# First norm by a root per quarter, delta-rule features by halves, differential attention's projections ahead of the grouped ones

## Chip, core and metric

The kernel runs on one core of a Trainium2 chip. The metric is the device time of one execution in microseconds; of three executions the median counts. TensorE is called PE here, VectorE DVE, ScalarE ACT, GpSimd POOL, and SP is the engine that issues all DMAs.

## What is computed

Two layers of a diffusion block with four mixers side by side, on 512 latent and 256 context tokens (768 in all) of width 1024, batch 1, in float32. The reference, cut to one layer:

```
mod_l = split(silu(c) @ mod_w + mod_b, 6);  mod_c likewise from c_ctx
h = rms_norm(x, g) * (1 + scale) + shift            # latent and context
pa, pb, pc, pd = split(h @ w_in)                    # 1152, 768, 800, 512 columns
oa = rwkv7_mixer(pa)     # delta rule, 4 heads of 64, both directions, context first
ob = diff_attention(pb)  # softmax(q1 k1) - lam * softmax(q2 k2), 4 heads, rope, norms
oc = gla_mixer(pc)       # gated linear attention in chunks of 64, both directions
od = gqa_mixer(pd)       # 4 query heads on 2 key heads
x = x + gate * (concat(oa, ob, oc, od) @ w_out)
x = x + gate2 * conv_ffn(modulate(x))               # 2816 wide, 3-tap convolution
```

The second layer gives no context output.

## The kernel before

Tokens lie along the free axis and features on the 128 partitions: x is eight blocks [128, 768]. Large products run as three products of rounded halves (high x high, high x low, low x high); `weights` (line 366) loads pieces of 512 KB into a ring of three stages, ACT rounds them (line 378) and POOL subtracts for the low half (line 379). All scratch in SBUF comes from 30 slabs of 1536 columns that `Arena` hands out while the program is being written: a [768] tile is half a slab. PSUM has eight banks, handed out in the same way.

The program of a layer is written by generators that `weave` (line 300) runs in turns: each yields an amount of time, scaled by PACE, and the one with the least goes next. For the mixers these are `rwkv` (delta rule), `gla`, `attentions`, `projections`, and in layer 0 `mod_mix`, the later modulation vectors. A generator may also wait for a flag (`wait`) or for whole free slabs (`room`). A scheduler then orders the instructions of each engine, so code order is not queue order; each engine takes its queue in order.

- **Start** (`start`, line 1840): x is loaded block by block, squared on ACT, and summed over the width by 48 products with the square as the weights and one column of ones (line 1849). The modulation vectors of shift and scale come in eight pairs; pair m is what block m of the norm needs (`mod_first`, `mod_pair`: line 466 the products on four column groups, line 470 the turn). `norm` calls pair m right before block m, then computes block m: DVE line 619, ACT line 621, and for the low half DVE line 623, or, for blocks 1, 4 and 7, ACT line 626 and POOL line 628. The first feature projections (line 388) follow block by block.
- **Projections** (line 756): gated linear attention's, the delta rule's, then the grouped keys and values, grouped queries, and differential keys, values and queries (line 748, per token tile 24 products). Raw keys, queries and values are spilled to DRAM (line 810). At the end h is freed and the flag "h free" is set.
- **Attentions**: `begin` (line 1041) waits for the kind's flag and for "h free", makes rope tables, loads six key tiles (line 936), turns them (POOL lines 884, 886, 890, DVE 887, 891), splits them (ACT 903, DVE 904) and transposes them on PE (line 428). Then scores (line 979, grouped 982), maximum (DVE 985), exponential (ACT 987), transposes and values (line 1015), unit by unit: differential pair 0, pair 1, grouped.
- **Delta rule**: `front(d)` waits for four whole slabs, then computes for each half p (two heads) the features (`features`: products with the small matrices at line 1390, DVE 1393 to 1416), into one slab KB with keys and b side by side and one slab RA. When both halves are there, `blocks` makes the 64x64 blocks per chunk pair (line 1434, ACT 1440, scratch writes 1443), and KB and RA are dumped (lines 1505, 1507). `inverses` (DVE 1463, 1465) works on the scratch; `direction` loads the dumps (1474, 1476) and runs `rw_prep` (line 1590) and `rw_chain` (1708, 1713) over six chunk pairs, whose POOL step is line 1622.

## Time and profile before

| what | value |
|---|---|
| median of three runs | 2402.65 us (2399.67 to 2406.67) |
| the profiled execution | 2396.04 us |
| its span, first to last instruction | 2394.1 us |
| PE busy | 2219.6 us (93%) |
| DVE, POOL, ACT busy | 1320.7, 994.7, 937.3 us |
| mean granted PE clock | 0.951 |
| PE line 388 (three-product projections, feed-forward) | 1235.9 us |
| PE line 748 (token projections) | 250.6 us |

The places of the two layers in the span: start to 82 us; projections of layer 0 to 382.7 us; its mixers to 755 us; output projection, feed-forward and the next norm to 1407 us; projections of layer 1 to 1701 us; mixers to 1973 us; the rest to the end.

A busy PE is one whose queue has a product under way; how fast it goes depends on the granted clock, which is given as a share of full speed. A wait is shown in brackets behind an instruction, with the engine and line that ended it. In the timeline the x counts are records: a product of float32 operands in one pass pair leaves two.

### The profile page before, as it was taken

To read this page: it belongs to the slowest core of one execution; us is meant where nothing else is said; L and a number is where in the kernel's file an instruction comes from. 1 tells how busy PE (TensorE), PEld (TensorE's weight loads), DVE (VectorE), ACT (ScalarE), POOL (GpSimd) and SP (SyncE) were. 2 spreads that over 40 slices of the span, in tenths; PEclk is the share of its full clock that TensorE was granted. 3 is DMA by queue.
4 is the path that set the end of the run, shared out by engine and by line. 5 is a ranking of instruction groups with operands and counts; after the bars stand their busy time and mean duration, and the time that the engine had idled before them with its cause. 6 is when DMAs were issued, how large, how long until landed. Compare 5 with 4: busy or idle time off the path is not lost. (4 is left out here: it accounts for less than half of the span.)

```text
span 2394.1 us, 40730 instructions
## 1 busy us (share of the span) xinstructions
PE 2219.6 (93%) x15684; PEld 1876.6 (78%) x15684; DVE 1320.7 (55%) x2902; ACT 937.3 (39%) x1762; POOL 994.7 (42%) x994
## 2 busy tenths in 40 slices
PE   7989995888989999999999989997899889999999
PEld 6778794767767788888888878777778668888888
DVE  2133567686784498555544662368767875332323
ACT  3333232545566342323223344322266474433333
POOL 1343445222431253434344545345442414655556
PEclk8999997789999999999999999998899899999999
DMA  6522254332324244333423432135533232333334
GB/s 217 202 80 85 80 178 119 94 76 63 84 88 146 86 133 130 112 107 115 141 93 102 150 103 65 56 96 143 124 92 80 60 124 80 97 97 97 97 97 133
DMA packets 228978, 258.52 MB, mean 108 GB/s; under 512 B 90608, under 2 KB 173872, under 8 KB 228784
## 3 DMA queue, kind: packets, MB, share of 16 engines
q1 hardware_dynamic: 228784, 255.92, 35.5%
q8 instruction: 123, 2.02, 0.3%
q14 instruction: 71, 0.58, 0.1%
HBM read 209.69 MB, written 37.77 MB: 103 GB/s over the span
## 5 line engine op out<-in xcount | busy, mean ns | idle before, releaser
L388 PE MATMUL pst<-slab,slab 128*128 128x512 f32 (+1 forms) x6552 | 1235.9, 350 | 13.1 <-POOL slab L628 5.4
L388 PEld LDWEIGHTS pst<-slab,slab 128*128 128x128 f32 x6552 | 1047.1, 190 | 196.0 <-POOL slab L628 10.0
L379 POOL TENSOR_TENSOR slab<-slab,slab 128x512 fp32r<-128x512 f32 (+1 forms) x428 | 566.6, 1333 | 718.4 <-ACT slab L378 686.7
L378 ACT CAST slab<-slab 128x512 fp32r<-128x512 f32 (+1 forms) x428 | 258.6, 612 | 570.7 <-PE pst L388 414.3
L748 PE MATMUL pst<-slab,slab 128*128 128x256 f32 (+1 forms) x1872 | 250.6, 293 | 4.2 <-POOL slab L379 4.0
L748 PEld LDWEIGHTS pst<-slab,slab 128*128 128x128 f32 x1872 | 239.6, 197 | 13.4 <-POOL slab L379 5.4
L428 PE MATMUL pst<-cst,slab 128*128 128x128 f32 (+1 forms) x968 | 170.1, 309 | 70.7 <-POOL slab L1622 23.9
L661 DVE SCALAR_TENSOR_TENSOR slab<-pst,pp,slab 128x511 f32<-128x511 f32 x66 | 41.6, 657 | 299.7 <-ACT slab L658 299.7
L428 PEld LDWEIGHTS pst<-cst,slab 128*128 128x128 f32 (+1 forms) x968 | 122.6, 155 | 100.7 <-POOL slab L1622 25.6
L1590 PE MATMUL pst<-slab,slab 128*128 128x128 f32 (+4 forms) x1328 | 162.8, 284 | 10.7 <-DMA slab<-kb 2.6
L1590 PEld LDWEIGHTS pst<-slab,slab 128*128 128x128 f32 (+3 forms) x1328 | 135.0, 180 | 33.0 <-issue 9.7
L692 DVE SCALAR_TENSOR_TENSOR slab<-pst,fgate,slab 128x512 f32<-128x512 f32 (+1 forms) x144 | 88.2, 628 | 108.0 <-PE pst L388 107.9
L985 DVE TENSOR_REDUCE mx<-pst 128x1 f32<-128x768 f32 (+1 forms) x120 | 100.1, 845 | 41.6 <-PE pst L979 27.2
L987 ACT ACTIVATE slab<-pst,mx 128x768 f32<-128x768 f32 (+1 forms) x120 | 97.8, 816 | 38.9 <-DVE mx L985 37.2
L532 DVE SCALAR_TENSOR_TENSOR slab<-slab,slab 128x512 bf16<-128x512 f32 x128 | 110.2, 861 | 4.7 <-DMA slab<-in_modw_dram 3.0
L673 POOL TENSOR_TENSOR slab<-slab,slab 128x768 fp32r<-128x768 f32 (+1 forms) x44 | 74.1, 1685 | 65.4 <-ACT slab L672 65.4
L1015 PE MATMUL pst<-slab,slab 128*64 128x128 f32 x832 | 67.7, 294 | 9.0 <-DVE slab L425 5.1
L998 ACT ACTIVATE slab<-slab,r 128x768 f32<-128x768 f32 (+1 forms) x80 | 67.1, 851 | 11.8 <-DVE r L997 11.6
L1015 PEld LDWEIGHTS pst<-slab,slab 128*64 128x64 f32 x832 | 48.0, 143 | 23.5 <-DVE slab L425 7.5
L672 ACT CAST slab<-slab 128x768 fp32r<-128x768 f32 (+1 forms) x44 | 32.1, 729 | 82.5 <-DVE slab L669 82.4
L667 ACT ACTIVATE slab<-slab 128x768 f32<-128x768 f32 (+1 forms) x44 | 32.5, 738 | 80.0 <-DVE slab L663 79.9
L1622 POOL TENSOR_TENSOR slab<-slab,pc 128x256 f32<-128x256 f32 x48 | 32.2, 686 | 67.8 <-PE pst L1708 14.6
(312 smaller groups left out, 2657.8 us busy)
## 6 DMA issues: line engine op xcount, KB each, us to landing
slab<-in_wup_dram SPq DMA_DIRECT2D x88, 512.0 KB, 3.7
slab<-in_modw_dram SPq DMA_DIRECT2D x112, 256.0 KB, 3.0
slab<-in_wdn_dram SPq DMA_DIRECT2D x48, 512.0 KB, 3.5
slab<-in_win_dram SPq DMA_DIRECT2D x46, 512.0 KB, 3.6
slab<-in_modp_dram SPq DMA_DIRECT2D x40, 512.0 KB, 5.1
slab<-in_wout_dram SPq DMA_DIRECT2D x16, 512.0 KB, 3.6
slab<-in_xT_dram SPq DMA_DIRECT2D x16, 384.0 KB, 5.0
kb<-slab SPq DMA_DIRECT2D x8, 768.0 KB, 4.0
```

What stands on the lines that cost most here:

```text
L378: nc.scalar.copy(out=w[0], in_=st[:, k:k + q])
L379: nc.gpsimd.tensor_tensor(out=w[1], in0=st[:, k:k + q], in1=w[0].bitcast(F32), op=ALU.subtract)
L388: self.nc.tensor.matmul(ps[:, a:b], w[i][k][:, cols], x[j][k][:, a:b], start=(k == 0 and q == 0), stop=(k == nk - 1 and q == 2))
L428: self.nc.tensor.transpose(out, a.bitcast(F32) if a.dtype != F32 else a, self.c["ident"])
L532: self.tc.keep_in_program_order(nc.vector.scalar_tensor_tensor(out=junk, in0=w, scalar=1.0, in1=self.sc[s][e], op0=ALU.mult, op1=ALU.mult, ...
L673: nc.gpsimd.tensor_tensor(out=HL[:, 1, :n], in0=th[:, :n], in1=HL[:, 0, :n].bitcast(F32), op=ALU.subtract)
L692: nc.vector.scalar_tensor_tensor(out=x[m][:, a:b], in0=ps[:, a:b], scalar=gate[:, m, s:s + 1], in1=x[m][:, a:b], op0=ALU.mult, op1=ALU.add)
L748: self.nc.tensor.matmul(ps[:, :n], h[i][k][:, t * P:(t + 1) * P], w[j][k], start=(k == 0 and q == 0), stop=(k == KD - 1 and q == 2))
L985: nc.vector.tensor_reduce(out=mx, in_=sv, axis=AX.XY, op=ALU.max, negate=True)
L987: nc.scalar.activation(out=p[m][:, a:].rearrange("p (e c) -> p e c", e=2 - a // hb), in_=sv, func=AF.Exp, bias=mx, accum_out=lsum[:, m:m + 1])
L1015: nc.tensor.matmul(acc[64 * e:64 * e + 64, :P], vs[e][:, i + j], aT[:, 256 * j + P * e:256 * j + P * e + P], start=(first and j == 0), sto ...
L1590: mm = lambda o, a, b, pos: nc.tensor.matmul(o, a, b, start=True, stop=True, tile_position=pos)
```

## The change

Four parts.

1. `start` sums the squares with 32 columns of ones as weights and the square moving, one product per quarter of the tokens, each on its own column group. `mod_first` runs all eight modulation pairs before the norm, with four pairs of buffers instead of three, and the first two projection weights are asked for before them. `root_first` computes the root on [128, 192] and spreads it with four products. For the other norms the same code as before moved into `root`.
2. `front` waits for nine free half slabs of which two are whole (`halves`), and does one half p after the other: features into four separate [768] tiles, blocks of this half, dumps of this half, and frees them.
3. `projections` does differential keys, values and queries first and the grouped ones last.
4. `begin` no longer waits for "h free"; the first one waits for five whole slabs.

```diff
-    ROOM = ((4, 7, 4, 2), (4, 7, 4, 2))
+    ROOM = (((9, 2), 7, 4, 2), ((9, 2), 7, 4, 2))
...
     def mod_first(self):
-        ws = [[self.new([4, 256]) for _ in range(2)] for _ in range(3)]
+        n = 4
+        ws = [[self.new([4, 256]) for _ in range(2)] for _ in range(n)]
...
+        self.early.update({q: self.win(0, q, 0, KD) for q in EARLY})
+        for m in range(KD):
+            ps = yield from self.bank(1, 2, 4)
+            self.mod_pair(m, [ws[m % n][k // 4][:, k % 4] for k in range(KD)], ps)
+            self.free(ps)
+            if m + n < KD:
+                load(m + n)
+        self.free(*sum(ws, []))
+
+    def root_first(self, ps):
+        n = T // 4
...
+        ms, r, t1, t2 = (self.new([n]) for _ in range(4))
+        nc.vector.tensor_scalar(out=ms, in0=ps[:, :n], scalar1=1.0 / D, scalar2=EPS, op0=ALU.mult, op1=ALU.add)
+        self.rsqrt(r, ms, t1, t2)
+        rb = yield from self.bank(4, 4, 8)
+        for g in range(4):
+            nc.tensor.matmul(rb[:, 512 * g:512 * g + n], first[32 * g:32 * g + 32], r[32 * g:32 * g + 32], start=True, stop=True,
+                             tile_position=(32 * g, 0))
+        rs = self.new([T])
+        nc.scalar.copy(out=rs.rearrange("p (g c) -> p g c", g=4), in_=rb.rearrange("p (g c) -> p g c", g=4)[:, :, :n])
...
-        for kind, hd, nh, nk, blocks in (("gq", 64, 4, 2, ("gqkv", "gqq")), ("da", 32, 8, 8, ("dak", "dav", "daq"))):
+        for kind, hd, nh, nk, blocks in (("da", 32, 8, 8, ("dak", "dav", "daq")), ("gq", 64, 4, 2, ("gqkv", "gqq"))):
...
+    def halves(self, n, slabs):
+        for _ in range(100000):
+            last, m = self.arena.last, Arena.SLAB // 2
+            free = [np.isfinite(last[:, q:q + m]).all(axis=1) for q in (0, m)]
+            whole = free[0] & free[1]
+            part = np.array([k == F32 for k in self.arena.kind])
+            if (whole * 2).sum() + ((free[0] ^ free[1]) & part).sum() >= n and whole.sum() >= slabs:
+                break
+            yield 100
...
-            yield from self.wait(S, kind + " ready", "h free")
+            yield from self.wait(S, kind + " ready")
+            if before is None:
+                yield from self.room(5)
...
-            nc.vector.tensor_tensor(out=KBp[:, :, 0:4:3], in0=ch2(tb), in1=ch2(ip), op=ALU.mult)
+            nc.vector.tensor_tensor(out=bx, in0=tb, in1=ip, op=ALU.mult)
...
-            nc.vector.tensor_tensor(out=KBp[:, :, 1:3], in0=ch2(th), in1=ch2(ip), op=ALU.mult)
+            nc.vector.tensor_tensor(out=kx, in0=th, in1=ip, op=ALU.mult)
...
+        def blocks(d, p, bx, rx):
+            ps = yield from self.bank(2, *self.RB[d])
+            for j in range(NT):
                 for hl in range(2):
+                    for u in range(2):
+                        nc.tensor.matmul(ps[U(u), 512 * hl + 64 * j:512 * hl + 64 * j + 64], rx[U(hl), j * P + 64 * u:j * P + 64 * u + 64],
+                                         bx[U(hl), j * P + 64 * u:j * P + 64 * u + 64], start=True, stop=True, tile_position=(64 * hl, 64 * u))
+            for hl in range(2):
+                ab = self.new([NT, 64])
+                nc.scalar.copy(out=ab.rearrange("p j t -> p (j t)"), in_=ps[:, 512 * hl:512 * hl + 64 * NT])
...
         def front(d):
-            KB[d], RA[d] = [], []
-            yield from self.room(self.ROOM[li][0])
             for p in range(2):
-                KB[d].append(self.new([NT, 4, 64]))
-                RA[d].append(self.new([2, T]))
-                yield from features(d, p)
+                yield from self.halves(*self.ROOM[li][0])
+                kx, bx, rr, rx = (self.new([T]) for _ in range(4))
+                yield from features(d, p, kx, bx, rr, rx)
+                yield from blocks(d, p, bx, rx)
...
+                nc.sync.dma_start(out=self.kb[d][:, :, p, 64:192], in_=kx.rearrange("p (j c) -> p j c", j=NT))
+                for u in range(2):
+                    nc.sync.dma_start(out=kbd[:, :, 3 * u], in_=c2(bx)[:, :, u])
+                for e, (a, m) in enumerate(((rr, nt), (rx, NT))):
+                    nc.sync.dma_start(out=self.ra[d][:, :m, p, e], in_=a[:, :m * P].rearrange("p (j t) -> p j t", j=m))
+                self.free(kx, bx, rr, rx)
...
-            ps = yield from self.bank(1, 4, 5)
+            ps = yield from self.bank(1, 0, 1)
...
-                for t in range(NT):
-                    nc.tensor.matmul(ps[:, t:t + 1], v[:, t * P:(t + 1) * P], self.c["ones"][:, 0:1],
-                                     start=(k == t == 0), stop=(k == KD - 1 and t == NT - 1))
+                for g in range(4):
+                    nc.tensor.matmul(ps[32 * g:32 * g + 32, 0:T // 4], self.c["ones"][:, 0:32], v[:, T // 4 * g:T // 4 * (g + 1)],
+                                     start=(k == 0), stop=(k == KD - 1), tile_position=(0, 32 * g))
...
-            yield from self.norm(0, "nmg", x, [st], h, [self.spans(True)], first)
+            yield from self.mod_first()
+            yield from self.norm(0, "nmg", x, [{}], h, [self.spans(True)], ps)
```

How the queues are ordered. PE at the start, before: line 1849 are the sums, 466 and 470 the modulation pairs, 604 the spread of the root, 388 the projections.

```order
L466 MATMUL pst<-slab_16_180,slab_5_100 32x256 x4
L466 MATMUL pst<-slab_17_181,slab_5_100 32x256 x4
L604 MATMUL pst<-slab_13_108,cst 128x512
L604 MATMUL pst<-slab_13_108,cst 128x256
L470 MATMUL pst<-cst,slab_5_100 128x2 x2
L466 MATMUL pst<-slab_18_182,slab_5_100 32x256 x4
L466 MATMUL pst<-slab_19_183,slab_5_100 32x256 x4
L466 MATMUL pst<-slab_20_184,slab_5_100 32x256
L470 MATMUL pst<-cst,slab_6_101 128x2 x2
L466 MATMUL pst<-slab_20_184,slab_5_100 32x256 x3
L466 MATMUL pst<-slab_21_185,slab_5_100 32x256 x4
L388 MATMUL pst<-slab_27_240,slab_1_96 128x512
```

PE at the same place, after (lines 1879, 470, 474, 514 and 392 are the same steps):

```order
L474 MATMUL pst<-cst,slab_7_102 128x2 x2
L470 MATMUL pst<-slab_18_166,slab_5_100 32x256 x4
L470 MATMUL pst<-slab_19_167,slab_5_100 32x256 x4
L474 MATMUL pst<-cst,slab_16_164 128x2 x2
L470 MATMUL pst<-slab_20_168,slab_5_100 32x256 x4
L514 MATMUL pst<-slab_6_101,slab_5_100 128x192 x4
L470 MATMUL pst<-slab_21_169,slab_5_100 32x256 x4
L474 MATMUL pst<-cst,slab_16_164 128x2 x2
L470 MATMUL pst<-slab_22_170,slab_5_100 32x256 x4
L392 MATMUL pst<-slab_25_319,slab_1_96 128x512
L392 MATMUL pst<-slab_25_319,slab_2_97 128x512
L392 MATMUL pst<-slab_25_319,slab_1_96 128x256
```

The spread of the root moved from behind the second pair to the middle of the seventh, and no projection stands before it.

SP in layer 0, before, from the spill of the last projected block: rawdaq is the spill of differential queries (line 810), slab<-rawdak a load of a key tile (line 936), scrin, kb and ra the delta rule's scratch and dumps.

```order
L810 DMA rawdaq<-slab_8_103 128x1536
L1480 DMA slab_6_101<-scrin_400 64x4x64 x2
L936 DMA slab_20_184<-rawdak 128x128 x2
L1505 DMA kb_89<-slab_17_181 768x1x256
L1507 DMA ra_91<-slab_16_180 768x1x128
L936 DMA slab_39_463<-rawdak 128x128
L1507 DMA ra_91<-slab_16_180 768x1x128
L936 DMA slab_98_3681<-rawdaq 128x128
L1676 DMA slab_108_3823<-slab_6_101 64x64 x4
L936 DMA slab_39_463<-rawdak 128x128
L1676 DMA slab_108_3823<-slab_6_101 64x64 x3
L936 DMA slab_98_3681<-rawdaq 128x128
```

SP in layer 0, after; rawgqq is the spill of the grouped queries (line 832), now the last block:

```order
L969 DMA slab_5_100<-rawdak 128x128
L1471 DMA scrin_388<-slab_6_101 64x6x64 x2
L1471 DMA scrin_388<-slab_33_385 64x6x64 x2
L969 DMA slab_7_102<-rawdak 128x128
L969 DMA slab_18_166<-rawdak 128x128
L1509 DMA slab_18_166<-scrin_387 64x4x64
L969 DMA slab_10_105<-rawdak 128x128
L969 DMA slab_90_3485<-rawdaq 128x128
L969 DMA slab_33_385<-rawdak 128x128
L969 DMA slab_115_3904<-rawdaq 128x128
L1509 DMA slab_21_169<-scrin_387 64x4x64
L832 DMA rawgqq<-slab_13_108 128x1536
```

The loads of the second to sixth key tile stand before that spill, behind the scratch writes of the second direction's first half.

PE in layer 1, before, around the last projection product (line 748); 1590, 1708 and 1713 are the delta rule's, 428 transposes of keys, 979 scores.

```order
L1590 MATMUL pst<-slab_16_180,slab_6_101 64x64 x7
L748 MATMUL pst<-slab_331_7199,slab_316_6633 128x256
L1708 MATMUL pst<-slab_385_12345 64x64 x4
L1590 MATMUL pst<-slab_356_10595,slab_35_398 64x128 x4
L1708 MATMUL pst<-slab_385_12345 64x64 x4
L1713 MATMUL pst<-slab_6_101,slab_373_11747 64x64 x4
L1590 MATMUL pst<-slab_18_182,slab_356_10595 128x128 x4
L1590 MATMUL pst<-slab_380_12310,slab_20_184 128x128 x4
L1590 MATMUL pst<-slab_356_10595,slab_18_182 128x64 x8
L428 MATMUL pst<-cst,slab_380_12310 128x2x64 x4
L428 MATMUL pst<-cst,slab_356_10595 128x128 x2
L1590 MATMUL pst<-slab_20_184,slab_376_12099 64x64 x8
```

PE in layer 1, after, where the first scores stand (line 1012); 770 are projections, 1620 the delta rule's.

```order
L770 MATMUL pst<-slab_330_7175,slab_314_6604 128x256
L432 MATMUL pst<-cst,slab_390_13745 128x128 x4
L1012 MATMUL pst<-slab_388_13736,slab_390_13745 128x384
L1012 MATMUL pst<-slab_389_13737,slab_390_13745 128x384
L1012 MATMUL pst<-slab_388_13736,slab_390_13745 128x384
L1012 MATMUL pst<-slab_389_13737,slab_390_13745 128x384 x2
L1012 MATMUL pst<-slab_388_13736,slab_390_13745 128x384
L1620 MATMUL pst<-slab_322_6989 128x64 x4
L1012 MATMUL pst<-slab_388_13736,slab_390_13745 128x384
L1012 MATMUL pst<-slab_389_13737,slab_390_13745 128x384
L770 MATMUL pst<-slab_212_5540,slab_315_6605 128x256
L770 MATMUL pst<-slab_329_7170,slab_315_6605 128x256
```

The last key transposes and the first scores stand in front of projection products, of which 168 more follow.

## Rows read from the trace of the kernel before

**Rows 1.** windows of the span; "x" are records, then clock, DMA share, GB/s:

```profile
core 0: us, PE busy (x) PEld busy (x) DVE busy (x) ACT busy (x) POOL busy (x), PEclk, DMA share, GB/s
10.00:15.00 5.00, 5.00 (x26) 5.00 (x25) 0.00 (x0) 1.68 (x2) 0.00 (x0) 1.00 1.03 413
28.50:82.00 53.50, 45.59 (x281) 28.47 (x281) 21.33 (x61) 20.51 (x43) 10.86 (x8) 0.84 0.59 202
382.70:433.00 50.30, 19.49 (x137) 14.56 (x138) 30.83 (x67) 10.52 (x25) 27.85 (x47) 0.56 0.38 110
433.00:755.00 322.00, 279.60 (x2616) 228.11 (x2617) 236.30 (x627) 183.48 (x402) 88.68 (x145) 0.92 0.34 92
755.00:1407.00 652.00, 640.57 (x3604) 553.91 (x3603) 390.04 (x734) 198.82 (x311) 275.24 (x189) 0.98 0.38 119
1595.50:1660.00 64.50, 47.79 (x433) 42.66 (x432) 46.90 (x93) 21.55 (x52) 43.06 (x45) 0.88 0.52 149
1701.00:1759.00 58.00, 46.27 (x306) 37.16 (x301) 37.88 (x105) 23.21 (x51) 21.78 (x43) 0.74 0.40 100
1759.00:1973.00 214.00, 196.87 (x1929) 161.29 (x1924) 160.95 (x393) 134.76 (x270) 67.09 (x114) 0.94 0.32 88
```

**Rows 2.** timeline of PE at the start (start us, us, instruction, wait):

```profile
7.92 20.64 PE L1849 MATMUL pst<-cst,slab 128*128 128x1 f32 x96 [7.92 <-ACT slab L1847]
...
76.98 1.82 PE L388 MATMUL pst<-slab,slab 128*128 128x512 f32 x8 [2.32 <-POOL slab L628]
```

**Rows 3.** timeline of DVE in the first norm:

```profile
49.31 1.15 DVE L619 SCALAR_TENSOR_TENSOR slab<-slab,gs,slab 128x512 f32<-128x512 f32 x2
50.85 1.15 DVE L623 SCALAR_TENSOR_TENSOR slab<-slab,mod,slab 128x512 fp32r<-128x512 f32 x2 [0.39 <-ACT slab L621]
...
59.52 1.15 DVE L619 SCALAR_TENSOR_TENSOR slab<-slab,gs,slab 128x512 f32<-128x512 f32 x2
...
64.46 1.15 DVE L619 SCALAR_TENSOR_TENSOR slab<-slab,gs,slab 128x512 f32<-128x512 f32 x2
```

**Rows 4.** timeline of PE at the end of layer 0's projections:

```profile
379.55 3.13 PE L748 MATMUL pst<-slab,slab 128*128 128x256 f32 x24
394.73 0.48 PE L428 MATMUL pst<-cst,slab 128*128 128x128 f32 x1 [12.06 <-POOL slab L1622]
...
432.89 0.97 PE L979 MATMUL pst<-slab,slab 128*128 128x384 f32 x4
```

**Rows 5.** timeline of PE in layer 1's projections:

```profile
1600.67 0.49 PE L1434 MATMUL pst<-slab,slab 64*64 64x64 f32 x8 [4.40 <-DVE slab L1411]
...
1648.18 0.49 PE L1434 MATMUL pst<-slab,slab 64*64 64x64 f32 x8 [8.17 <-DVE slab L1411]
```

**Rows 6.** DMA issues: form, count, KB each, median us to landing:

```profile
kb<-slab SPq DMA_DIRECT2D x8, 768.0 KB, 4.0
...
scrin<-slab SPq DMA_DIRECT2D x48, 64.0 KB, 2.4
```

**Rows 7.** groups of instructions by form, 382.7 to 455 us: count, busy, mean ns, idle:

```profile
L884 POOL TENSOR_TENSOR slab<-slab,slab 128x64 f32<-128x64 f32 x12 | 3.9, 340 | 8.2 <-DMA slab<-rawdak 4.3 <-DMA slab<-rawdaq 1.9 <-DVE slab L425 1.7
...
L886 POOL TENSOR_TENSOR slab<-slab,slab 128x128 f32<-128x128 f32 x6 | 2.8, 474 | 0.5
```

**Rows 8.** timeline of DVE and POOL in the inverses of layer 0:

```profile
357.44 0.42 DVE L1465 TENSOR_TENSOR slab<-slab,slab 96x252 f32<-96x252 f32 x1
...
358.13 1.33 POOL L379 TENSOR_TENSOR slab<-slab,slab 128x512 fp32r<-128x512 f32 x1 [1.68 <-issue]
358.34 1.39 DVE L1465 TENSOR_TENSOR slab<-slab,slab 96x247 f32<-96x247 f32 x1
```

**Rows 9.** timeline of PE in layer 1's attention:

```profile
1759.75 0.66 PE L1015 MATMUL pst<-slab,slab 128*64 128x128 f32 x8
...
1764.19 0.66 PE L428 MATMUL pst<-cst,slab 128*128 128x128 f32 x4
...
1775.64 0.62 PE L979 MATMUL pst<-slab,slab 128*128 128x384 f32 x2
```

119 lines of the change are left out of this document (47 added, 72 removed).

## Prediction

> **What bounds the kernel now.** I read the profile by stages: first the busy table of the stretches, then, in each stretch where TensorE (PE) is not filled, the PE timeline with the releaser of each wait. The stretches to look at are those in which PE has work left and does not do it [rows 1]. From 28.5 to 82 us it is busy for 45.59 of 53.50 us; from 382.7 to 433 us for 19.49 of 50.30 us at a granted clock of 0.56; from 1595.5 to 1660 us for 47.79 of 64.50 us; from 1701 to 1759 us for 46.27 of 58.00 us at 0.74. The stretch from 755 to 1407 us, mostly feed-forward, is full at 640.57 of 652 us, and the change does not touch it. So I price three places and take everything else as it was.
>
> Why PE is short of work differs by place. At the start the first 28.5 us go to the sums of squares, 96 records of single-column products over 20.64 us (a product in this type leaves two records) [rows 2]; after that the eight blocks of the first norm come one by one, and the last run of feature products ends at 76.98 + 1.82 = 78.8 us [rows 2]. In layer 0 the last projection ends at 379.55 + 3.13 = 382.7 us and the first scores of attention stand at 432.89 us [rows 4]: keys are loaded, turned and transposed only after all projections, and PE sits 12.06 us for a GpSimd product and then creeps. In layer 1 there are two waits for the delta rule's features (4.40 and 8.17 us, [rows 5]) and again the hole behind the projections.
>
> **The change part by part. The start.** Removed: 48 products that load 128 columns of weights to move one column, 20.64 us of PE. Added: 32 products of 32 weight columns and 192 moving ones, which stand on separate column groups. The change gives PE so little here that the loads decide: constants 612 + 187 + 8 KB, eight x blocks of 384 KB, sixteen halves of modulation weights of 512 KB and two of projection weights, 13.4 MB in one queue by the shapes in the code. At the rate that the queue reaches, 413 GB/s from 10 to 15 us [rows 1], they take 32.5 us; with about 2 us before the first packet and 2 to land, the first half of the seventh pair, behind which PE now holds the matmul that spreads the root, is there at about 33 us, and the root is in SBUF at about 36 us. Moved: all eight modulation pairs now precede the norm, so each block no longer waits for a pair. What is late next is the block's own chain, for its buffer y is still a single one: 49.31 to 50.85 + 1.15, that is 2.7 us, for a block finished on VectorE, and 59.52 to 64.46, 4.9 us, for one that goes over GpSimd [rows 3]. Five of the first and three of the second are 28.2 us: 36 + 28 = 64 us, and with the last block's products about 66 us instead of 78.8. That is 12.8 us. Two small things remain: some of the next projection's products now stand between the last blocks (a gain of up to 4 us), and PE enters this stretch with little behind it; the granted clock of 28.5 to 82 us was 0.84 [rows 1], and a stretch at the lower of its two levels, 1.2 GHz, would cost about as much. I take **-13 us**; if loads get three quarters of that rate, -3, and if the overlap comes free of charge, -19.
>
> **Layer 0's projections.** Differential attention's three blocks now come first, and its begin no longer waits for h to be freed, only for five whole slabs. In the order, key loads stand ahead of the last spill of the grouped projections, GpSimd's rotations stand ahead of the last two squares, and the 24 key transposes stand directly behind the last projection. So the stretch of 50.3 us is what goes. Its PE work at full clock is 19.49 x 0.56 = 10.9 us. Behind it, from 433 to 755 us, PE did 279.60 x 0.92 = 257 us of work in 322, a rate of 0.80. At this rate the whole 268 us take 335 us, and I add 8 us: most key loads stand on SP's queue behind the scratch writes of the second direction's first half, so they start only some 12 us before the last projection ends, and per tile GpSimd needs two products of 0.34 us and one of 0.47, six tiles being 7 us [rows 7], with VectorE and ScalarE steps behind. 343 against 372 us: **-28 us**, rounded down. Bounds: nothing added, -37; a lead as long as 25 us, -12. The grouped keys are not needed before both pairs of differential heads are done, so their delay is hidden.
>
> **The delta rule by halves.** Per direction, 12 small copies on ScalarE become 4 of 384 columns, 12 scratch writes become 8, and the features are written to buffers of their own, so VectorE's strided writes become plain ones. The number of block products is unchanged. Added: dumps of the features go from 6 to 10 issues per direction, and 1536 x 2 of their pieces are 256 bytes. The nearest rows are a dump of 768 KB in 1 KB pieces, 4.0 us, and a scratch write of 64 KB in 256-byte pieces, 2.4 us [rows 6]; per half this bounds the landing between 4 and about 8 us, and who waits is the first load of prepared chunks, many us later, behind the inverses. I take 0. The two waits in layer 1 [rows 5] become four points where PE's queue holds block products behind 48 to 96 projection products; the same VectorE chain stands before each. Each point has less ahead of it than before, but the block needs one half only. Between -12 and +12 I take 0.
>
> The Trainium skill (DMA: Bandwidth & Descriptors, Specifications) speaks against this part: below 512 bytes a transfer does not reach line rate, since it is read, modified and written. By that rule the two dumps of 192 KB per half would take about twice their time on the queue, an estimate of some 2 us more per half; no row here separates pieces by size, and it would change the sum only where a weight load stands right behind them, by 0 to 4 us per layer.
>
> **Layer 1's projections.** Here the order goes further: behind the last block products, 13 pieces of attention (28 score products, 28 value products, 78 transposes) stand between the 240 grouped projection products, which thus cover their waits. By rows: 28 x 0.5 us (a lone score product is 0.62), 28 x 2 records at 0.66 per 8, and 66 more transposes at 0.66 per 4 [rows 9], less 24 fewer chunk products of about 5 us: 14 + 4.6 + 10.9 - 5 = 24.5 us of work that moves ahead of the projections' end. From 1701 to 1973 us PE does 46.27 x 0.74 + 196.87 x 0.94 = 219 us of work in 272. With 195 us left at the rate of 1759 to 1973, 0.865, the tail is 225 us, and 24.5 + 225 - 272 = -22 us. Against it stand waits inside the 13 pieces; the stretch of 382.7 to 433 us has eleven waits in its 30.8 idle us [rows 1, 4], 2.8 us on average; covered by projections I take 0.8 each, 10 us. **-12 us**, between -24 and +15. What is late next is the delta rule: its main run now starts only after the projections, with attention already ahead, and both end together.
>
> A second rule, first as the trace has it: a VectorE product of 252 elements took 0.42 us, and the next, of 247, took 1.39 us while a GpSimd product that had begun 0.21 us earlier ran for 1.33 us [rows 8]. The Trainium skill (SBUF — State Buffer, SBUF: two separate sides) says that a GpSimd instruction and a VectorE one with two SBUF inputs exclude each other for a whole instruction. The trace agrees. By it, the key rotations that now run beside the inverses would hold VectorE for at most their own 7 us per layer, which layer 0's projections cover and layer 1's block products would not.
>
> **The sum.** -13 - 28 + 0 - 12 = -53 us. The profiled execution took 2396.04 us with a span of 2394.1; the median of the runs is 2402.65, 6.6 us above. I apply the difference to the median: 2402.65 - 53 = **2350 us** (2343 on the profiled scale).
>
> **The rivals.** (a) *Layer 0's keys still come late.* SP's queue holds the loads until the second direction's features are through; if these slip, the lead is 25 us or more and the grouped projections end with nothing ready. For it speaks that four of the six first loads stand behind scratch writes; against it that the projections then last another 72 products. -13 - 10 - 12 = -35: 2368 us.
> (b) *The delta rule becomes layer 1's end.* Its serial chain, started behind the attention pieces and with VectorE shared as in [rows 8], runs no faster than before: layer 1 comes out at +15. For: it starts later and attention no longer outlasts it. Against: from 1759 to 1973 us PE was busy 197 of 214 us, so the chain was paced by PE, which has less to do now. -13 - 28 + 15 = -26: 2377 us.
> (c) *All three places at their better end*, -19 - 37 - 24 = -80: 2323 us.
> (d) *Slower.* PE takes its queue in order; in layer 1 each of the 13 pieces that waits for a rotation or an exponential stops the projections that were meant to cover it. Price: 13 times the wait. At the 2.8 us of the hole it is 36 us and the sum is -27; from 0.8 + 53/13 = 4.9 us each nothing is left, and at 6 us the kernel is at 2417 us. For: key transposes stand one projection tile behind the last query products. Against: only the first pieces are so close.
> (e) *The change does not do what it says*: five slabs are free only when h is, both holes stay, and only the start is left: 2390 us. Against: the order shows the loads early.
>
> **How the numbers follow.** Forecast 0.54, (a) 0.12, (b) 0.12, (c) 0.12, (d) 0.05, (e) 0.05. Range: the forecast, (a), (b) and (c) with some spread of their own, eight in ten: 2316 to 2386 us. A measurement of this kernel can tell about 0.3%, 7.2 us, from no change: faster is below 2395.4. The forecast, (a), (b), (c) and half of (e) are faster, with something off for an unseen cause: 0.89; same 0.05; slower 0.06.
>
> **What would show it.** Start: the last feature products of the first norm end near 66 us, blocks 2.7 and 4.9 us apart. Layer 0: first scores within 20 us of the last projection, no stretch at half clock there. Layer 1: scores between projections, granted clock near 1 from the features on, the last chunk products and the last scores ending together. It is wrong if block products wait over 10 us in layer 1, if the projections end over 40 us later, relative to the features, than before, or if the feed-forward parts change length.

## The result, and the profile after

The changed kernel takes 2372.49 us (median of four runs, 2366.77 to 2375.56) against 2401.16 us of the kernel before: a ratio of 0.9881, with an interval from 0.9862 to 0.9900. In a later comparison it took 2370.92 against 2395.93 us, 0.9889 (0.9866 to 0.9913). So the change gives 25 to 29 us. I had forecast -53 us and 2350 us; the time lies in the range that I gave, the gain is half of what I forecast.

The profiled execution took 2371.69 us, with a span of 2369.8 us against 2394.1. I cut both spans at the same six places in the work: the end of the 100th token product, in each layer the end of the last projection and the first product of the output projection, and the first token product of layer 1. The windows of before at these cuts, columns as in [rows 1]:

```profile
99.90:382.70 282.80, 273.09 (x2351) 234.04 (x2349) 133.70 (x306) 88.66 (x161) 122.99 (x118) 0.98 0.35 107
382.70:753.30 370.60, 297.41 (x2744) 241.45 (x2744) 265.43 (x693) 193.33 (x426) 116.53 (x192) 0.87 0.34 93
753.30:1407.10 653.80, 642.35 (x3610) 555.21 (x3611) 391.84 (x735) 199.58 (x312) 275.24 (x189) 0.98 0.38 120
1407.10:1701.50 294.40, 267.25 (x2198) 231.56 (x2197) 162.76 (x362) 102.95 (x199) 141.57 (x137) 0.96 0.32 90
1701.50:1974.10 272.60, 243.52 (x2229) 198.79 (x2228) 198.84 (x497) 158.37 (x322) 88.87 (x156) 0.89 0.33 90
```

The same windows after, and with them the stretch from the last projection of layer 0 to its first scores, which answers to the hole of 50.30 us in [rows 1]:

```profile
86.10:385.90 299.80, 279.85 (x2399) 240.12 (x2397) 138.52 (x316) 88.96 (x155) 127.50 (x127) 0.95 0.35 106
385.90:418.90 33.00, 16.82 (x107) 13.43 (x107) 26.34 (x57) 8.97 (x20) 22.82 (x35) 0.60 0.37 102
385.90:726.20 340.30, 293.72 (x2697) 238.73 (x2697) 263.12 (x683) 191.53 (x415) 111.69 (x183) 0.90 0.36 95
726.20:1379.60 653.40, 640.70 (x3612) 553.41 (x3611) 390.40 (x736) 199.82 (x314) 273.67 (x189) 0.99 0.39 121
1379.60:1717.60 338.00, 288.95 (x2301) 248.86 (x2301) 208.81 (x475) 128.53 (x233) 157.16 (x176) 0.93 0.30 83
1717.60:1948.40 230.80, 208.56 (x2126) 175.34 (x2127) 153.84 (x387) 131.29 (x271) 74.26 (x118) 0.94 0.37 103
```

Read down the lengths. The start is 13.8 us shorter (99.9 to 86.1). Then layer 0's projections are 17.0 us longer, which I had not expected at all, and what follows them in layer 0 is 30.3 us shorter. The feed-forward part is the same (653.8 and 653.4). Layer 1's projections are 43.6 us longer, since attention's work now stands among them, and the rest of the layer is 41.8 us shorter: together +1.8. With 1.4 us more behind layer 1, this is the 24.3 us between the spans. Against my terms: the start as forecast, layer 0 at -13.3 instead of -28, layer 1 at +1.8 instead of -12.

Where PE waits at the end of layer 0's projections, to be held against [rows 4] (start, duration, instruction, wait):

```profile
382.75 3.13 PE L770 MATMUL pst<-slab,slab 128*128 128x256 f32 x24
390.74 1.11 PE L432 MATMUL pst<-cst,slab 128*128 128x128 f32 x4 [4.86 <-DVE slab L937]
...
397.08 3.03 PE L432 MATMUL pst<-cst,slab 128*128 128x128 f32 x13 [3.41 <-DVE slab L937]
401.57 1.12 PE L432 MATMUL pst<-cst,slab 128*128 128x128 f32 x4 [1.46 <-DVE slab L937]
...
416.41 1.12 PE L432 MATMUL pst<-cst,slab 128*128 128x128 f32 x4 [2.51 <-DVE slab L937]
...
418.89 1.34 PE L1012 MATMUL pst<-slab,slab 128*128 128x384 f32 x4
```

The 12.06 us for GpSimd are gone, but the first scores stand 33 us behind the last projection, not the 20 that I gave, and at a clock of 0.60. And in layer 1, to be held against [rows 5]:

```profile
1620.81 1.56 PE L1465 MATMUL pst<-slab,slab 64*64 64x64 f32 x48 [10.10 <-DVE slab L1443]
...
1631.62 3.14 PE L1547 MATMUL pst<-rk,slab 128*128 128x2 f32 x14 [3.07 <-POOL slab L1454]
1641.82 1.12 PE L432 MATMUL pst<-cst,slab 128*128 128x128 f32 x4 [7.06 <-DVE slab L937]
```

Before there were 4.40 and 8.17 us; now one wait of 10.10 for the last features, and behind it a new one of 7.06 for the first turned key. Two of the signs that I had named for being wrong are there: block products that wait over 10 us, and projections that end over 40 us later relative to the features (96.8 us behind the last block products, 1620.81 to 1717.6, against 53.3 before, 1648.18 to 1701.5).

### The profile page after: what moved, and what is told of

It reads as the page before. It is cut to its first block, busy times and chain, and to the rows that moved or that the text cites. A ratio compares the mean times of both kernels' runs of the same rounds, so it can differ in the third digit from the quotient of the medians.

```text
span 2369.8 us, 40603 instructions
## 1 busy us (share of the span) xinstructions
PE 2194.0 (93%) x15656; PEld 1852.1 (78%) x15656; DVE 1327.0 (56%) x2900; ACT 934.2 (39%) x1730; POOL 995.9 (42%) x999
## 5 line engine op out<-in xcount | busy, mean ns | idle before, releaser
L432 PE MATMUL pst<-cst,slab 128*128 128x128 f32 (+1 forms) x968 | 166.4, 305 | 69.1 <-DVE slab L937 21.7
L432 PEld LDWEIGHTS pst<-cst,slab 128*128 128x128 f32 (+1 forms) x968 | 120.6, 153 | 96.6 <-DVE slab L937 24.3
L551 DVE SCALAR_TENSOR_TENSOR slab<-slab,slab 128x512 bf16<-128x512 f32 x104 | 92.2, 886 | 5.1 <-DMA slab<-in_modw_dram 3.5
L1012 PE MATMUL pst<-slab,slab 128*128 128x384 f32 (+1 forms) x144 | 48.8, 407 | 14.0 <-ACT slab L1020 6.4
```

The source lines that it names most:

```text
L432: self.nc.tensor.transpose(out, a.bitcast(F32) if a.dtype != F32 else a, self.c["ident"])
L551: self.tc.keep_in_program_order(nc.vector.scalar_tensor_tensor(out=junk, in0=w, scalar=1.0, in1=self.sc[s][e], op0=ALU.mult, op1=ALU.mult, ...
```

## The experiments

**Each part alone.** The first question was which part made which piece of this. Three kernels hold one part each.

Only the start (part 1):

> The kernel before with the first part of the change alone (sums by quarters, all modulation pairs ahead of the norm). Theory A, the start is a gain of its own that reaches the end: the 100th token product ends 13 to 15 us earlier than before (99.9 us there), the last projection of layer 0 the same 13 to 15 us earlier, the kernel at 2387 us. Theory B, the start costs layer 0's projections what it gains, since banks and buffers are handed out in another order (after the whole change they take 17 us longer, 10 of them idle): the 100th product comes 14 us earlier, the last projection only 0 to 7 us earlier, the kernel at 2394 to 2401 us.

Measured: 2393.93 us against 2399.54, a ratio of 0.9986 (0.9964 to 1.0008). The 100th token product ends at 86.5 us, 13.4 us earlier; the last projection at 380.5 us, 2.2 us earlier. Theory B: most of the start's gain is gone before layer 0's projections end. (This profiled execution took 2399.68 us, 5.8 above the median.)

Only the halves (part 2):

> The kernel before with the second part alone (delta rule's features, blocks and dumps by halves). Theory A, by halves is worth nothing by itself: 2401 us, within 7. Theory B, the halves free the first direction's inverses sooner, VectorE takes them ahead of the second direction's features, and PE waits for these: a wait of 8 to 12 us before the fourth run of block products in layer 1, up to 10 us more idle time within layer 0's projections, 2405 to 2418 us. Theory C, the halves let the delta rule start sooner and shorten both layers: 2385 to 2393 us.

Measured: 2394.39 us against 2399.54, 0.9984 (0.9965 to 1.0003). The sum is theory A's; the pieces are not. In layer 0 what follows the projections is 342.8 us instead of 370.6, nearly all that the whole change wins there; in layer 1 the projections and mixers take 582.8 us instead of 567.0. (This profiled execution was 9.5 us below its median, so some of the first figure is luck.)

Only attention first (parts 3 and 4):

> The kernel before with the third and fourth parts alone (differential attention's projections first, its start no longer behind the freeing of h). Theory A, this part alone makes the gain in layer 0's hole: from the last projection to the first scores about 33 us instead of 50, 13 to 30 us off layer 0, nothing in layer 1: 2372 to 2388 us. Theory B, without the halves there are not five free slabs before h is freed, so attention cannot start early and the order of the blocks alone changes little: 2394 to 2405 us. Theory C, without the halves nothing holds the key rotations up on VectorE, and layer 1 gains its 12 us too: 2355 to 2370 us.

Measured: 2434.34 us against 2399.54, 1.0148 (1.0121 to 1.0174): slower by 35 us, which no theory had. Its layer 1, projections and then the rest:

```profile
1403.70:1756.00 352.30, 293.75 (x2259) 253.29 (x2258) 208.80 (x463) 128.30 (x246) 158.27 (x166) 0.88 0.27 78
1756.00:2004.90 248.90, 216.88 (x2169) 181.07 (x2167) 157.74 (x398) 134.87 (x274) 74.25 (x127) 0.94 0.35 98
```

58.55 us of the projections are idle (352.30 less 293.75; 27.15 before) and the clock falls to 0.88. In its PE timeline block products of the old form wait 5.69, 8.09 and, alone, 11.64 us:

```profile
1644.50 0.49 PE L1436 MATMUL pst<-slab,slab 64*64 64x64 f32 x8 [8.09 <-DVE slab L1413]
...
1666.85 0.47 PE L1436 MATMUL pst<-slab,slab 64*64 64x64 f32 x2 [11.64 <-ACT slab L1442]
...
1684.34 4.03 PE L428 MATMUL pst<-cst,slab 128*128 128x128 f32 x16 [4.36 <-DVE slab L904]
```

The delta rule's serial chain starts at 1803.3 us there (1701.4 before) and ends at 1984.3, with attention at 1989.4. It resembles my rival (d), PE stopped by the order of its queue, but not in what waits: (d) had attention's pieces, and of the 31 us more idle time these three waits are 25.4, where before two such waits were 12.6; the waits for keys and scores are no longer than with the whole change. Why the block products come so late here was not tested by a run of its own.

**The parts in pairs.** The three parts alone sum to +24 us, together they give -25 to -29. So some 50 us come from their meeting. Two more kernels leave out one part each.

Without attention first (start and halves):

> The changed kernel without its third and fourth parts (start and halves alone; grouped projections first, attention behind the freeing of h). The parts alone gave -6 us (start), -5 us (halves) and +35 us (attention first), together -29: somewhere 50 us come from their meeting. Theory A, attention first pays only where the halves have freed the slabs and moved the delta rule ahead, and then it is worth what I forecast in layer 1: layer 1 is 10 to 16 us longer here than with the whole change (568.8 us there), layer 0 about as long (640 us), the kernel at 2382 to 2392 us. Theory B, the halves carry the gain in layer 0, and attention first, with them, is worth nothing: 2366 to 2376 us. Theory C, the parts' order in the queues is what differs, and start and halves simply add up: 2387 to 2390 us with both layers as in the run of the halves alone (631 and 583 us).

Measured: 2401.64 against 2397.20 us, 1.0024 (1.0009 to 1.0038), slower than each theory had. Layer 0 takes 646.0 us, layer 1 590.7.

Without the start (halves and attention first):

> The changed kernel without its first part (the start as before, with halves and attention first). Theory A, the start gives its 13.5 us where the end of the kernel sees it: 2386 us. Theory B, as the start alone gave only 6 of its 13.5 us to the end, it does so here: 2376 to 2380 us. In either case attention first with the halves, without the start, is at least 10 us faster than before, which the part alone was not (2434 us).

Measured: 2390.41 against 2397.20 us, 0.9972 (0.9952 to 0.9992). Theory B is out: here the start is worth 18 us and more, where alone it gave 6, so more than the 13.5 of theory A too. Attention first, which alone cost 35 us, does not with the halves, but the gain over before is 7 us and not the 10 that I expected in either case. In the profiles the start is worth 13.5 us here (spans of 2383.3 and 2369.8): 3.8 by the end of layer 0, and 10.4 in layer 1 (579.2 against 568.8), whose code it does not touch.

The pieces of all these kernels, cut as above, in us (profiled executions; the changed kernel twice, so that one sees that layer 0 repeats to 4 us and layer 1 to 1):

| kernel | median less before | start | layer 0: projections | rest | layer 1: projections | rest |
|---|---|---|---|---|---|---|
| before | | 99.9 | 282.8 | 370.6 | 294.4 | 272.6 |
| start | -5.6 | 86.5 | 294.0 | 362.9 | 299.5 | 279.2 |
| halves | -5.2 | 96.4 | 288.6 | 342.8 | 305.4 | 277.4 |
| attention first | +34.8 | 99.2 | 299.3 | 349.7 | 352.3 | 248.9 |
| start, halves | +4.4 | 86.0 | 295.2 | 350.8 | 302.1 | 288.6 |
| halves, attention first | -6.8 | 100.4 | 292.2 | 337.4 | 324.3 | 254.9 |
| all | -28.7 | 86.1 | 299.8 | 340.3 | 338.0 | 230.8 |
| all, again | -25.0 | 86.5 | 298.9 | 337.3 | 339.8 | 228.0 |

Two things are read from it. In layer 0 the halves and attention first shorten the same piece, by 28 and 21 us alone and by 33 together, and each makes the projections longer. In layer 1 each of them alone costs (582.8 and 601.2 us against 567.0), and all three together do not (568.8). What attention first is worth thus depends on what stands beside it: by medians +35 us alone, -2 on the halves, and -29 to -33 on start and halves. Which wait makes this difference is not settled. The profiled executions lie up to 9.5 us below and 5.8 above the medians of their kernels, so differences of a few us in single pieces say nothing.

**Layer 1 as before.** Does early attention pay there?

```diff
-            yield from self.wait(S, kind + " ready")
-            if before is None:
+            yield from self.wait(S, kind + " ready", *(["h free"] if li else []))
+            if before is None and not li:
                 yield from self.room(5)
...
-        ... in (("da", 32, 8, 8, ("dak", "dav", "daq")), ("gq", 64, 4, 2, ("gqkv", "gqq"))):
+        ... in (("da", 32, 8, 8, ("dak", "dav", "daq")), ("gq", 64, 4, 2, ("gqkv", "gqq")))[::-1 if li else 1]:
```

> The changed kernel with the third and fourth parts undone in layer 1 alone: grouped projections first there, and attention behind the freeing of h. Theory A, the early attention in layer 1 has an own gain of about 12 us that another cost of the halves in layer 1 hid: layer 1 takes 578 to 585 us (568.8 with the whole change), the kernel 2382 to 2390 us. Theory B, the early attention in layer 1 is worth nothing, its waits eat what it moves: layer 1 takes 565 to 573 us, the kernel 2368 to 2377 us. Theory C, it costs: below 565 us, 2360 to 2367 us.

Measured: 2383.09 against 2397.20 us, 0.9947 (0.9933 to 0.9962). Layer 1 takes 304.2 + 272.8 = 577.0 us, 8 more than with the whole change: nearest theory A, a little below the layer's time that I gave for it, with the kernel's time inside. The 8 us are no pure price of early attention, though. The kernel of start and halves has the same code for layer 1, and there the layer takes 590.7 us (302.1 and 288.6, here 304.2 and 272.8). Even PE's waits in its projections are others: 23.3 us for rounded weights there, and here 3.2 for those and 13.28 for block products. So what the rest of a kernel does to buffers and order moves layer 1 by more than these 8 us. In its profile the delta rule's last output stands at 1888.3 us and attention's last value product at 1952.7, so attention has the last 64 us to itself; in the changed kernel they end at 1929.4 and 1932.9.

**Which wait ate the start's gain.** In the changed kernel a wait of PE in layer 0 has no counterpart before: a feature projection that waits for VectorE's eviction of an earlier one. These projections take two of four PSUM banks, the two that have been free longest. In the program of before the first five pairs in this place are (1,2), (0,1), (2,3), (1,2), (0,1), in that of the changed kernel (2,3), (1,2), (0,1), (2,3), (0,1): the start takes its banks otherwise, and so other neighbours share a bank. The second and third matter: in both kernels VectorE evicts the second only behind a step of gated linear attention (at 224.46 us before, 210.50 after). Before, the third, (2,3), shared no bank with it; now (0,1) shares bank 1 with (1,2). PE's timeline of the changed kernel, of the start alone, and of the kernel with the edit below:

```profile
212.45 7.85 PE L392 MATMUL pst<-slab,slab 128*128 128x256 f32 x33 [3.90 <-DVE slab L818]
```
```profile
215.60 7.29 PE L392 MATMUL pst<-slab,slab 128*128 128x256 f32 x33 [7.34 <-DVE slab L818]
```
```profile
197.76 14.50 PE L392 MATMUL pst<-slab,slab 128*128 128x512 f32 x82
```

The edit lets a feature projection begin at an even bank only, so that two following ones share none:

```diff
-    def bank(self, n, lo, hi):
+    def bank(self, n, lo, hi, step=1):
...
-            for b in range(lo, hi - n + 1):
+            for b in range(lo, hi - n + 1, step):
...
-        ps = yield from self.bank(2, 0, hi)
+        ps = yield from self.bank(2, 0, hi, 2)
         self.mm_feat(ps, w, h, segs)
```

> The changed kernel with one edit: a feature projection of the mixers takes two PSUM banks that begin at an even number, so that two following ones never share a bank. Theory A, the 3.9 us that PE waits at 212 us for VectorE's eviction (7.3 us in the run of the start alone, none in the kernel before) come from two following projections that share a bank: the wait is gone and layer 0's projections end 4 to 8 us earlier than in the changed kernel (385.9 us), the kernel at 2364 to 2370 us. Theory B, the token products, which take single banks out of the same four, then wait instead, or the orders of later stages change by as much: 2370 to 2382 us.

Measured: 2366.26 us, 0.9880 (0.9857 to 0.9902) of a kernel before of 2397.20: theory A's time, with layer 0's projections ending at 379.8 us, 6.1 earlier, but by ratio no different from the changed kernel, which had run beside another set of runs. So both ran together:

> The changed kernel once more, beside the next run, since 6 us between them are less than two sets of runs on different chips can tell. Every theory: 27 to 32 us below the kernel before, stages as in its first profile (86, 640, 653, 569 us).

> The changed kernel with projections on pairs of PSUM banks that begin at an even number, beside the changed kernel. Theory A, the wait that this takes away in layer 0 (3.9 us and 3.1 us of slower clock after it in the first profiles) reaches the end: 5 to 8 us below the changed kernel. Theory B, the 6 us between the first medians were chance: within 3 us of it.

Measured: 2370.92 us for the changed kernel, 25 us below before and not the 27 to 32 expected; 2362.88 for the pairs, 0.9857 (0.9836 to 0.9878) of before: 8 us lower, theory A. The intervals of the two ratios still touch, but no run of the pairs in this set (2362.64 to 2368.18 us) is as slow as the changed kernel's median. The windows of the stretch from the first to the last products of gated linear attention's chunks say where: before, changed, pairs.

```profile
172.70:275.00 102.30, 102.30 (x929) 82.40 (x929) 34.52 (x79) 29.48 (x48) 33.79 (x31) 1.00 0.22 73
```
```profile
158.70:268.00 109.30, 105.40 (x931) 85.14 (x931) 34.99 (x79) 29.56 (x48) 34.19 (x31) 0.97 0.21 69
```
```profile
158.40:260.60 102.20, 102.20 (x922) 82.18 (x922) 34.58 (x75) 29.48 (x48) 34.49 (x32) 1.00 0.21 71
```

The wait of 3.90 us costs 7.0: the other 3.1 are the same products at a clock that fell from 1.00 to 0.97. Right behind the wait, in the changed kernel, PE is busy at half clock (1.2 GHz):

```profile
212.00:218.00 6.00, 5.55 (x22) 5.29 (x23) 0.69 (x2) 0.62 (x1) 6.00 (x6) 0.50 0.26 82
```

The same edit on the start alone:

> The kernel before with the first part of the change and even pairs of banks. Theory A, the start alone gave back its 13.4 us in layer 0 because projections came to share a bank (a wait of 7.34 us at 215.6 us): that wait is gone, the last projection of layer 0 ends at 369 to 374 us (380.5 without the pairs, 382.7 before), the kernel 9 to 14 us below the kernel before, 2384 to 2389 us. Theory B, the gift back has another cause: the last projection stays at 377 to 382 us, the kernel at 2391 to 2396 us.

Measured: 2382.07 against 2395.93 us, 0.9925 (0.9901 to 0.9949), 13.9 us faster; the last projection of layer 0 ends at 373.0 us. Theory A: with the pairs the start is worth what it saves. (The profiled execution is 9.3 us below the median, so the stage figure flatters it a little.) The pairs on top of the whole change are the fastest kernel of this study.

**The waits in layer 1's projections.** The 10.10 us stand where VectorE goes through the first direction's inverses (L1492, L1494 in the timeline) among the steps of the second direction's features. First, both directions' features ahead of the inverses in layer 1:

```diff
-            if d:
+            if d and not li:
                 yield from front(1)
                 yield from bonus()
...
         yield from front(0)
+        if li:
+            yield from front(1)
+            yield from bonus()
         gens = [direction(d) for d in range(2)]
```

> The changed kernel with one edit: in layer 1 both directions' features stand ahead of the first direction's inverses. Theory A, the 10.1 us that PE waits before the fourth run of block products in layer 1 come from the inverses on VectorE, which stood between and ahead of the features: the wait falls below 4 us and the kernel gains 5 to 12 us, 2361 to 2368 us. Theory B, the wait only moves: the inverses now stand between the key rotations and hold up the key transposes (7.1 us now, then 10 to 18), or the delta rule ends later than attention: 2372 to 2385 us.

Measured: 2392.30 against 2399.54 us, 0.9965 (0.9948 to 0.9981), some 20 us slower than the changed kernel. The wait of the block products is gone, but the key transposes now wait 11.88 us (7.06), and PE waits five times, 2.5 to 4.6 us each, among the projections for rounded weights, whose loads stand on SP behind the features' scratch writes and dumps. Theory B in kind, and slower than its range. Then the inverses' work itself left out, in layer 1:

```diff
+                if li:
+                    yield 2.1 * m * w + 200
+                    continue
                 z = tm[:q, :m * w].rearrange("p (m w) -> p m w", m=m)
```

> The changed kernel without VectorE's products and sums of the inverses in layer 1 (124 instructions, 51.5 us of VectorE; the output is not the reference's). Theory A, these set the two largest waits in layer 1's projections, 10.10 us before the fourth run of block products and 7.06 us before the first key transposes: both fall below 3 us, and layer 1 is 12 to 25 us shorter than the 568.8 us of the changed kernel. Theory B, the features' own chain over ScalarE, VectorE and GpSimd sets the first wait and GpSimd's rotations the second: each loses less than half, layer 1 is shorter by less than 8 us.

Measured: 2383.71 against 2395.93 us, 0.9939 (0.9914 to 0.9964); its layer 1 takes 344.2 + 224.7 = 568.9 us, as with the inverses (568.8). Its PE timeline:

```profile
1633.63 1.56 PE L1465 MATMUL pst<-slab,slab 64*64 64x64 f32 x48 [4.80 <-DVE slab L1443]
1643.16 3.15 PE L1550 MATMUL pst<-rk,slab 128*128 128x2 f32 x14 [7.98 <-POOL slab L1454]
1650.35 2.82 PE L432 MATMUL pst<-cst,slab 128*128 128x128 f32 x12 [4.03 <-DVE slab L937]
```

The two waits shrink by about half (10.10 to 4.80, 7.06 to 4.03), not below 3 us as theory A had it, but the one for GpSimd between them grows from 3.07 to 7.98, and the layer is no shorter, as theory B had it. From 1617 to 1650 us GpSimd is busy 25.56 of 33 us: with VectorE out of the way, it is next. So the inverses place the waits and, in this profile, do not set their sum: PE is idle for 52.0 us of these projections, 49.05 with the inverses. (The kernel's median is 12.8 us above that of the changed kernel beside it, and its profiled execution is the fastest of its five. That execution is 2.8 us longer in span than the changed kernel's first, and none of it is in layer 1. Where the slower executions lose time is not known.)

## Why the prediction was right and wrong

**The start, -13 us: right in size, wrong about what follows.** -13.8 measured. The products that spread the root stand at 37.07 us, and the first scaling with it begins at 39.07; I had the root in SBUF at 36. The last products of the first norm end at 72.5, not 66: 3 of the 6 us are that, the others slower blocks. The scaling of two halves took 1.15 us on VectorE and 2.23 beside GpSimd's low halves of the next projection's weights, which came only now into this stretch.

```profile
48.39 1.15 DVE L641 SCALAR_TENSOR_TENSOR slab<-slab,gs,slab 128x512 f32<-128x512 f32 x2 [2.64 <-POOL slab L650]
...
58.43 2.23 DVE L641 SCALAR_TENSOR_TENSOR slab<-slab,gs,slab 128x512 f32<-128x512 f32 x2
```
```profile
58.36 2.96 POOL L383 TENSOR_TENSOR slab<-slab,slab 128x288 fp32r<-128x288 f32 x3
```

The Trainium skill (SBUF — State Buffer, SBUF: two separate sides) has such a pair exclude each other for whole instructions; these rows agree, as [rows 8] did, and I had put that rule at the inverses and not here. The 6 us did no harm, since token products already stood between the last blocks. The step that failed is the sentence with which I began: price three places and take everything else as it was. The bank pairs moved, and 7 of the 13.8 us were lost at a line that the change does not touch.

**Layer 0, -28 us: the size of one piece right, its cause and the piece ahead of it wrong.** The rest of the layer is 30.3 us shorter, where I had 372 to 343, that is 29. That the sizes agree is luck: I credited it to attention first and gave the halves nothing. Halves alone take 28 us from this piece (12 on top of the start, 362.9 to 350.8); attention first alone takes 21 and pays most of it back in the projections. The hole itself shows it: from the last projection to the first scores it is 33.5 us with the halves alone (385.0 to 418.5), where attention still waits for h, and 33.0 with the whole change. With halves the delta rule, too, comes sooner: in that run its chain starts at 432.2 us instead of 458.9.

Why 33 us and not the 20 that I gave: I priced the keys and not the queries. All six key tiles are transposed by 402.7 us, 17 us behind the last projection. The query tile that the first scores take is turned on GpSimd (L917), and there it stands behind products of the delta rule's features (L1446), which wait for VectorE:

```profile
404.18 1.81 POOL L1446 TENSOR_TENSOR slab<-slab,slab 128x768 f32<-128x768 f32 x1 [4.36 <-DVE slab L1445]
...
410.39 1.31 POOL L917 TENSOR_TENSOR slab<-slab,slab 128x64 f32<-128x64 f32 x2
```

The projections ahead of it are 17.0 us longer: 7.0 by the bank, and 10.2 from 268 us on (117.9 against 107.7), where idle time is some 7 us more and the clock 0.94 instead of 0.97. The largest single wait there is a modulation turn:

```profile
356.90 1.02 PE L474 MATMUL pst<-cst,slab 128*128 128x2 f32 x4 [4.27 <-ACT slab L472]
```
```profile
355.48 0.84 ACT L1430 ACTIVATE slab<-slab 128x768 f32<-128x768 f32 x1 [6.58 <-DVE slab L1428]
356.23 0.35 ACT L852 COPY slab<-pst 128x256 f32<-128x256 f32 x1
356.48 0.38 ACT L472 COPY slab<-pst 128x256 f32<-128x256 f32 x1
```

PE waits for a copy on ScalarE (L472) that is queued behind the exponential of the features (L1430), which waits 6.58 us for VectorE's scan. It also stands in both kernels with halves that I read there without attention first (4.14 and 4.49 us), and not in that of the start alone, so it comes with the halves. I had named who is behind VectorE's features on PE, not on ScalarE.

**The delta rule by halves, 0: right in the sum by two errors.** Alone it is -5.2 us (not told from none), but as a gain in layer 0 and a cost in layer 1: 15.8 us alone, 12 on top of the start (590.7 against 578.7), 10 in the kernel with layer 1 as before (577.0 against 567.0). The cost is in part weights that come late: in the run of the halves PE waits for their low halves 2.99, 4.97, 5.75, 3.62 and 2.36 us in layer 1's projections (2.19 and 1.83 before), as loads stand on SP behind scratch writes and dumps that wait for the features. In the kernel with layer 1 as before it is not that, as PE waits only 3.2 us for weights there; what its 10 us are is open. As for the dumps of short pieces, the page's groups of the changed kernel:

```profile
kb<-slab SPq DMA_DIRECT2D x16, 192.0 KB, 3.7
kb<-slab SPq DMA_DIRECT2D x8, 384.0 KB, 3.3
```

In the median 192 KB in 256-byte pieces take longer to land than 384 KB in 512-byte pieces, but most of these dumps are issued within 1 us of another on the same queue; the quickest land after 2.5 and 3.1 us. The Trainium skill (DMA: Bandwidth & Descriptors, Specifications) has transfers below 512 bytes off line rate; these times neither show that nor speak against it. Whether the weights would have come in time with other pieces was not tried.

**Layer 1, -12 us: the wait inside the attention pieces was mis-sized, and the start of the sum was another.** The tail is 230.8 us against my 225, and PE's busy time in the projections rose by 21.7 us against 24.5 of work that I counted. Their idle time rose by 21.9 us (27.15 to 49.05) where I had put 10 for the 13 pieces: the waits before attention's key transposes, scores and values sum to 20.3 us, that is 1.6 per piece and not 0.8, and 7.06 of it is the first one. Another 3.07 us are for GpSimd ahead of them. Of the 14 us between forecast and result, some 10 are these waits and 6 the tail. Against layer 1 as before in a kernel that has the halves, the early attention is worth 8 us, near what I had, but that comparison is loose, as said above; against the kernel before it is eaten by what the halves cost there. That the delta rule and attention end together (1929.4 and 1932.9 us) was forecast and holds. What sets the length of layer 1's projections now is not settled: neither the order of the features nor the inverses' time on VectorE shortened it.

**The rivals.** The time came out near (a), 2368 us. Its condition was half there: four of the six key loads are issued only 9.2 to 3.8 us before the last projection ends (the second at 376.69 us) and one 2 us behind it, no key is split by then, and the lead is over its 25 us.

```profile
376.69 0.67 SPq L969 DMA_DIRECT2D slab<-rawdak  x1
```

But the price that (a) put on this did not follow: the rest of the layer is 30 us shorter all the same. (b) is true in its place, both ending together, but not as a loss of 15 us, and its chain does not run as slowly as before: it starts at 1761.8 us, 60 later than before, and takes 166.5 us instead of 218.3, as the argument against (b) had it. (d) is in part what happened, at 1.6 us for each of the 13 pieces.

## What to carry to other kernels

Where a scheduler and rotating buffers set the order, an edit acts where the code is untouched: run each part alone and without the others before adding their gains, and look for waits that have no counterpart before. Two edits that fill the same hole do not add up, and edits that each cost alone can cost nothing together: the layer 1 that takes 567.0 us before takes 582.8 and 601.2 with one of them, and 568.8 with all. Ask, for each engine that is held up, which small step of another stream is queued behind on it: here a copy on ScalarE, the turn of a query tile on GpSimd, and weight loads on SP.

## What was not expected of the hardware

- A wait of 3.90 us lowered the granted clock of the 109.3 us around it from 1.00 to 0.97, and the same products took 3.1 us more; with the wait gone the stretch was back at 102.2 us and 1.00. In the run of the start alone a wait of 7.34 us cost no more on top: 104.66 us of busy time at 0.97, 2.4 us more than before.
- Runs of one program scatter more than the effects in question: 25 runs of the kernel before lay between 2386.73 and 2410.12 us, and the pieces of layer 0 of the changed kernel differ by 4 us between two profiles. A few of the stage figures above rest on single profiles and are to be read to some 5 us.
